# Batched rotary q·k scores on one core: twenty 2 MB loads change from SyncE's DMA ring to ScalarE's

## The chip, the cores and the metric

The kernel runs on one core of a Trainium2 chip (trn2). The metric is device time in microseconds, the median of three runs. The kernel before takes 792.87 us (792.67 to 793.26). A difference is read against that spread.

Words used below: PE is TensorE, DVE is VectorE, ACT is ScalarE, POOL is GpSimd, SP is SyncE. A DMA is issued by an instruction on SP, ACT or POOL, which puts it on that engine's ring (a queue); the core's 16 DMA engines then move the data. The profile calls SP's ring q1, ACT's q10 and POOL's q0. "To landing" is the time from the issue of a DMA until its last byte has arrived.

## The reference

For 16 batches of 512 positions, 16 heads and 64 elements, q and k are rotated with cos and sin of the position, and for every batch and head all 512 x 512 products are written out:

```python
q1, q2 = q[..., :half_dim], q[..., half_dim:]
q_rot = np.concatenate([q1 * cos_q - q2 * sin_q, q1 * sin_q + q2 * cos_q], axis=-1)
...
scores = np.einsum('bshd,bthd->bsht', q_rot, k_rot)
```

q and k are 33.5 MB each in fp32, the scores 268.4 MB. The kernel reads 67.24 MB and writes 268.44 MB, so four fifths of its traffic are stores.

## The kernel before

A batch is cut into C = 4 chunks of 128 positions (positions p*4 + c for chunk c), and each step i of 64 makes the scores of one chunk of q against all 512 positions of k of its batch. A step writes one staging tile st of 128 x 16 x 512 fp32 (4 MB) from eight pairs of heads. For each pair (`scores`, L190 on) PE makes two matrices of 128 x 512 in PSUM (L201), and ACT copies both to st (L208). After the eighth pair, SP issues the store of the whole tile (L188). There are three staging tiles, so the copies of step i can begin only when the store of step i - 3 has landed.

The inputs arrive by batch: `load` (L113) takes a tile of 128 x 4 x 1024 fp32 (2 MB) from `in_pool`, which has two buffers for q and two for k, and issues the load into it (L122). DVE rotates one chunk at a time in place (`rope`, L149, L150 and L154). PE transposes it by 128 x 128 blocks (L170). DVE copies the transposed q out of PSUM, and ACT the transposed k (L185).

The order of the work on each engine is the order in which the program issues it (`manual_schedule`). The first four steps have a loop of their own, with smaller loads and stores. From step 4 on, one step is:

```python
for p in range(HP):
    scores(i, p, st)
    ...
run(dve)
if i % C == C - 2:
    load("q", i // C + 2)
elif i % C == C - 1:
    load("k", i // C + 3)
```

Between the pairs of heads stand the transposes: at p = 1 and 3 those of q for step i + 1, at p = 5 and 6 those of k for step i + 4. So in each group of four steps one q load is issued after the third step's store and one k load after the fourth's, all on SP, behind the stores of the steps before. A load may be issued when PE has transposed the last chunk of the batch that was in its buffer; that happens within the step that the load follows, before its last pair of heads.

Five loads (q of batches 6, 11, 15 and k of batches 7 and 12) are special (`RELIEVED`, `load_around`, L86 on): POOL issues 120 of their 128 partitions so that one DMA engine is passed over. The other 8 partitions go by SP (L111, for q) or POOL (for k). The tiny transfers into `scratch` (L84) only move POOL's place among the DMA engines.

Of the kernel before, what the change touches and what calls it, by code (L numbers as in the profile page):

```python
# [10 lines left out]
def kernel(  # L11
# [8 lines left out]
    nc = tc.nc  # L20
# [4 lines left out]
    B, S, H, D = q.shape  # L25
    HD = D // 2
    P = 128
    C = S // P
# [14 lines left out]
    dram = {  # L43
        "q": q.rearrange("b (p c) h d -> b p c h d", c=C),
        "k": k.rearrange("b (p c) h d -> b p c h d", c=C),
    }
# [15 lines left out]
    def load_units(which, head, heads):  # L62
        n = C * heads * D
        t = early[:, used[0] : used[0] + n].rearrange("p (c e) -> p c e", c=C)
        used[0] += n
        src = dram[which][0, :, :, head : head + heads, :]
        nc.sync.dma_start(t.rearrange("p c (h d) -> p c h d", d=D), src)
        for h in range(0, heads, G):
            units[which, (head + h) // G] = t[:, :, D * h : D * (h + G)]
# [16 lines left out]
    def load_around(which, b, t):  # L86

        n, E, F = 120, C * H * D, C * H * D // 2  # L90
        x = RELIEVED[which, b]
        d = dram[which][b]

        def halves(lo, hi):
            src = bass.AP(d.tensor, d.offset + lo * E + F, [(E, hi - lo), (-F, 2), (1, F)])
            v = t[lo:hi].rearrange("p c e -> p (c e)")
            dst = bass.AP(v.tensor, v.offset + F, [v.ap[0], (-F, 2), (1, F)])
            nc.gpsimd.dma_start(dst, src)  # L98

        if x == 0:  # L100
            nc.gpsimd.inc_swdge_sem([], [], mode="reset_dge_cursor")
        else:

            move_cursor(16 - SLOW)
        if x % 2:
            move_cursor(8)
            halves(n, P)
        move_cursor(SLOW + 1)
        halves(0, n)
        if not x % 2:  # L110
            nc.sync.dma_start(t[n:].rearrange("p c (h d) -> p c h d", h=H), d[n:])  # L111

    def load(which, b):  # L113

        if b >= B:
            return
        t = in_pool.tile([P, C, H * D], fp32, tag=which + "_in", name=which + "_sb")
        batches[which, b] = t
        if (which, b) in RELIEVED:
            load_around(which, b, t)  # L120
        else:
            nc.sync.dma_start(t.rearrange("p c (h d) -> p c h d", h=H), dram[which][b])  # L122

    def rope(which, n):

        part = part_pool.tile([P, H * D], fp32, tag="part", name="part")
        if n < C:
            x = units[which, n]
            sv, k1, k2 = "p c (g j) -> p c g j", {"j": HD}, {"j": D}  # L130
            cs = cos_t.unsqueeze(2).to_broadcast((P, C, 2 * G, HD))
            ss = ss_v.unsqueeze(2).to_broadcast((P, C, G, D))
            pv = part.rearrange("p (c g j) -> p c g j", c=C, j=D)
            x5 = x.rearrange("p c (h x j) -> p c h x j", x=2, j=HD)
            p5 = part.rearrange("p (c h x j) -> p c h x j", c=C, x=2, j=HD)
            adds = [(x5[:, :, :, y], p5[:, :, :, 1 - y]) for y in range(2)]
        else:
            x = batches[which, n // C][:, n % C]
            sv, k1, k2 = "p (g j) -> p g j", {"j": HD}, {"j": D}
            cs = cos_t[:, n % C].unsqueeze(1).to_broadcast((P, 2 * H, HD))  # L140
            ss = ss_v[:, n % C].unsqueeze(1).to_broadcast((P, H, D))
            pv = part.rearrange(sv, **k2)
            x4 = x.rearrange("p (h x j) -> p h x j", x=2, j=HD)
            swapped = bass.AP(part.tensor, part.offset + HD, [part.ap[0], (D, H), (-HD, 2), (1, HD)])
            adds = [(x4, swapped)]
        xs, xc = x.rearrange(sv, **k2), x.rearrange(sv, **k1)

        def products():
            nc.vector.tensor_tensor(pv, xs, ss, op=mult)  # L149
            nc.vector.tensor_tensor(xc, xc, cs, op=mult)  # L150

        def sums():
            for y, z in adds:
                nc.vector.tensor_tensor(y, y, z, op=add)  # L154

        return [products, sums]
# [33 lines left out]
    def scores(i, p, st):  # L190

        ps = ps_s_pool.tile([P, 2, S], fp32, tag="ps_s", name="ps")
        b = i // C
        if b == 0:
            c, hp = divmod(p, 2)
            lhs, rhs = qT[i][:, C * hp + c], kT[0][:, 2 * i + hp]
        else:
            lhs, rhs = qT[i][:, p], kT[b][:, p]
        for r in range(2):
            po, rh = ps[:, r, :], rhs[64 * r : 64 * r + 64, :]  # L200
            nc.tensor.matmul(  # L201
                out=po, lhsT=lhs[64 * r : 64 * r + 64, :], rhs=rh, start=True, stop=True
            )
        so, si = st[:, 2 * p : 2 * p + 2, :], ps
        if b > 0:
            so = so.rearrange("s r (t c) -> s r t c", c=C)
            si = si.rearrange("s r (c t) -> s r t c", c=C)
        nc.scalar.copy(out=so, in_=si)  # L208
        if b == 0 and p % 2 == 1:
            c = p // 2  # L210
            nc.sync.dma_start(o_v[0, c, :, G * i : G * (i + 1)], st[:, G * c : G * (c + 1)])
        elif b > 0 and p == HP - 1:
            store(i, st)

    def tr_act(which, n):
        for g in range(2):
            transposed(which, n, g, nc.scalar.copy)

    def run(ops):
        for op in ops:  # L220
            op()

    with tc.manual_schedule():
        for t, src in ((cos_t, cos), (sin_t, sin)):
            nc.scalar.dma_start(t, src.rearrange("(p c) j -> p c j", c=C))
        for head, heads in ((0, G), (G, H - G)):
            load_units("k", head, heads)
            load_units("q", head, heads)
        load("k", 1)
        load("q", 1)  # L230
        make_identity(nc, ident)
        nc.scalar.copy(out=ss_t[:, :, 0, :], in_=sin_t)
        nc.scalar.mul(ss_t[:, :, 1, :], sin_t, -1.0)
        for which in ("k", "q"):
            run(rope(which, 0))
            tr_act(which, 0)

        for i in range(C):
            st = st_first[i] if i < 2 else stage_pool.tile([P, H, S], fp32, tag="stage", name="st")  # L240
            if i < C - 1:
                dve = rope("k", i + 1) + rope("q", i + 1) + rope("k", C + i)
                nxt = [("k", i + 1), ("q", i + 1)]
            else:
                dve = rope("q", C) + rope("k", C + i) + rope("q", C + 1) + rope("k", 2 * C)
                nxt = [("q", C), ("k", C + i)]
            for p in range(HP):
                scores(i, p, st)
                if p in (0, 1) and i > 0:
                    run(dve[:1])  # L250
                    dve = dve[1:]
                    transposed("k", C + i - 1, p, nc.vector.tensor_copy)
                if p == 3 and i < 2:
                    load("kq"[i], 2)
                if p in (2, 6):
                    m = len(dve) - (4 if p == 2 else 2) - (2 if i == C - 1 else 0)
                    run(dve[:m])
                    dve = dve[m:]
                    tr_act(*nxt.pop(0))
            run(dve)  # L260
        load("k", 3)

        for i in range(C, NST):
            tr = {}
            if i + 1 < NST:
                tr[1], tr[3] = ("q", i + 1, 0), ("q", i + 1, 1)
            if i + C < NST:
                tr[5], tr[6] = ("k", i + C, 0), ("k", i + C, 1)
            dve = []  # L270
            if i + 2 < NST:
                dve += rope("q", i + 2)
            if i + 1 + C < NST:
                dve += rope("k", i + 1 + C)
            st = stage_pool.tile([P, H, S], fp32, tag="stage", name="st")
            for p in range(HP):
                scores(i, p, st)
                if p not in tr:
                    continue
                if tr[p][0] == "q":  # L280
                    run(dve[:1])
                    dve = dve[1:]
                    transposed(*tr[p], nc.vector.tensor_copy)
                else:
                    transposed(*tr[p], nc.scalar.copy)
            run(dve)
            if i % C == C - 2:
                load("q", i // C + 2)
            elif i % C == C - 1:
                load("k", i // C + 3)  # L290

# [28 lines left out]
```

## Time and profile before

| what | value |
|---|---|
| median of three runs | 792.87 us |
| span of the profiled execution, first to last instruction | 790.4 us |
| median less span | 2.5 us |
| PE busy | 684.4 us (87%) |
| ACT busy | 562.0 us (71%) |
| DVE busy | 544.7 us (69%) |
| POOL busy | 11.9 us (2%) |
| moved by DMA | 336.18 MB, mean 425 GB/s |
| issues on SP: stores of 4 MB (L188) | 60, median 24.7 us to landing |
| issues on SP: k loads and q loads of 2 MB (L122) | 13 and 12, median 28.3 and 26.5 us to landing |
| issues on POOL: q and k of 1920 KB | 3 and 2, median 27.8 and 43.3 us to landing |

How to read it: busy time says how much an engine ran, not whether its work was what the end waited for. An engine that waits part of the time but is late with nothing costs nothing. The DMA part of a page gives the busy share of the 16 DMA engines and what they moved, in 40 equal slices of 19.76 us. The waits give, for each engine and line, how long it sat idle and what ended that. A table by stretches gives the same sums between two chosen moments. Issuing a DMA isn't counted as busy time of the engine that issues it; its duration stands in the timeline, as a row of SPq or ACTq.

### The profile page before, as it was taken

How to read it: one execution, taken by the hardware profiler on the slowest of the kernel's cores; microseconds unless marked ns; L12 is line 12 of the kernel's file. 1: busy time of each engine (PE TensorE's matmuls, PEld its weight loads, DVE VectorE, ACT ScalarE, POOL GpSimd, SP SyncE). 2: the span in 40 equal slices, each digit the busy share in tenths (PEclk: the TensorE clock that was granted, in tenths of full speed). 3: DMA queues.
4: the chain of work that ended last, by engine and by line, in shares of the span. 5: the costliest groups of instructions: out<-in, count | busy, mean ns of one | idle time of the engine just before them, and what ended most of it. 6: DMA issues, size and time to landing. Idle time of an engine off the chain costs nothing.

```text
span 790.4 us, 7750 instructions
## 1 busy us (share of the span) xinstructions
PE 684.4 (87%) x3072; PEld 296.4 (38%) x3072; DVE 544.7 (69%) x516; ACT 562.0 (71%) x647; POOL 11.9 (2%) x24
## 2 busy tenths in 40 slices
PE   4989998988988889798996989889899798799960
PEld 2444443433433334343342433334334343344420
DVE  6999988666766678576785767667678487587400
ACT  3888886865857768486785866777577586588770
POOL 0000000000001000000000001000000000000000
PEclk9999999998999999898998989999899899899995
DMA  9999999999999999999999999999999999999997
GB/s 357 417 425 439 429 430 435 425 435 436 429 429 428 413 432 419 433 423 438 433 427 436 426 432 429 422 432 424 430 432 427 436 429 432 430 432 434 432 429 340
DMA packets 18836, 336.18 MB, mean 425 GB/s; under 512 B 2312, under 2 KB 3592, under 8 KB 4616
## 3 DMA queue, kind: packets, MB, share of 16 engines
q1 hardware_dynamic: 16704, 325.46, 96.4%
q0 software_dynamic: 1808, 10.10, 3.1%
q8 instruction: 24, 0.39, 0.2%
q10 hardware_dynamic: 288, 0.13, 0.1%
q14 instruction: 12, 0.10, 0.0%
HBM read 67.24 MB, written 268.44 MB: 425 GB/s over the span
## 4 chain that ended last, share of the span: by engine, by line
DMA 49%; PE 40%; ACT 5%; DVE 3%; issue 1%; ACTq 0%; SPq 0%; DVEq 0%
DMA out_dram<-st 46%; PE ps L201 30%; PE bank L170 10%; ACT st L208 5%; DMA q_sb<-in_q_dram 2%; DVE part L149 1%; DMA early<-in_k_dram 1%; DVE q_sb L150 0%; DVE k_sb L154 0%; DVE k_sb L150 0%; DVE q_sb L154 0%; DVE early L150 0%; DVE kT_t L185 0%; ACTq L316 0%; DVE early L154 0%
## 5 line engine op out<-in xcount | busy, mean ns | idle before, releaser
L208 ACT COPY st<-ps 128x1024 f32<-128x1024 f32 x512 | 495.7, 1020 | 192.6 <-DMA out_dram<-st 109.8
L201 PE MATMUL ps<-kT_t,qT_t 64*128 64x512 f32 x2048 | 544.0, 649 | 67.0 <-ACT st L208 67.0
L201 PEld LDWEIGHTS ps<-kT_t,qT_t 64*128 64x128 f32 x2048 | 183.6, 196 | 256.2 <-issue 133.3
L185 DVE COPY qT_t<-bank 128x512 f32<-128x512 f32 x118 | 81.6, 691 | 193.9 <-PE bank L170 193.9
L170 PEld LDWEIGHTS bank<-ident,q_sb 128*128 128x128 f32 x480 | 54.2, 149 | 99.0 <-issue 96.4
L170 PEld LDWEIGHTS bank<-ident,k_sb 128*128 128x128 f32 x480 | 50.3, 140 | 96.4 <-DVE k_sb L150 39.5
L170 PE MATMUL bank<-ident,q_sb 128*128 128x128 f32 x480 | 85.1, 304 | 0.9 <-PE ps L201 0.9
L170 PE MATMUL bank<-ident,k_sb 128*128 128x128 f32 x480 | 78.5, 286 | 1.6 <-DVE qT_t L185 1.2
L185 ACT COPY kT_t<-bank 128x512 f32<-128x512 f32 x122 | 72.4, 598 | 6.4 <-PE bank L170 6.4
L154 DVE TENSOR_TENSOR k_sb<-k_sb,part 128x1024 f32<-128x1024 f32 x60 | 73.5, 1225 | 2.1
L150 DVE TENSOR_TENSOR q_sb<-q_sb,cos_t 128x1024 f32<-128x1024 f32 x60 | 73.5, 1225 | 2.1
L150 DVE TENSOR_TENSOR k_sb<-k_sb,cos_t 128x1024 f32<-128x1024 f32 x60 | 73.5, 1225 | 2.0
L149 DVE TENSOR_TENSOR part<-q_sb,ss_t 128x1024 f32<-128x1024 f32 x60 | 73.5, 1225 | 2.0
L149 DVE TENSOR_TENSOR part<-k_sb,ss_t 128x1024 f32<-128x1024 f32 x60 | 73.0, 1216 | 0.9 <-DMA k_sb<-in_k_dram 0.7
L154 DVE TENSOR_TENSOR q_sb<-q_sb,part 128x1024 f32<-128x1024 f32 x60 | 72.9, 1216 | 0.0
L170 PE MATMUL bank<-ident,early 128*128 128x128 f32 x64 | 10.5, 315 | 12.4 <-DVE early L154 10.5
L170 PEld LDWEIGHTS bank<-ident,early 128*128 128x128 f32 x64 | 8.3, 161 | 17.4 <-issue 13.4
L149 DVE TENSOR_TENSOR part<-early,ss_t 128x1024 f32<-128x1024 f32 x8 | 9.8, 1222 | 5.8 <-DMA early<-in_k_dram 5.7
L98 POOL DMA_DIRECT2D q_sb<-in_q_dram x3 | 2.3, 752 | 620.2 <-PE bank L170 446.2
L154 DVE TENSOR_TENSOR early<-early,part 128x512 f32<-128x512 f32 x16 | 10.3, 687 | 0.2
L150 DVE TENSOR_TENSOR early<-early,cos_t 128x1024 f32<-128x1024 f32 x8 | 9.8, 1225 | 0.3
L185 ACT COPY qT_t<-bank 128x512 f32<-128x512 f32 x10 | 5.7, 629 | 3.2 <-PE bank L170 3.2
(12 smaller groups left out, 15.9 us busy)
## 6 DMA issues: line engine op xcount, KB each, us to landing
out_dram<-st SPq DMA_DIRECT2D x60, 4096.0 KB, 24.7
k_sb<-in_k_dram SPq DMA_DIRECT2D x13, 2048.0 KB, 28.3
q_sb<-in_q_dram SPq DMA_DIRECT2D x12, 2048.0 KB, 26.5
out_dram<-st SPq DMA_DIRECT2D x16, 1024.0 KB, 13.8
q_sb<-in_q_dram POOLq DMA_DIRECT2D x3, 1920.0 KB, 27.8
k_sb<-in_k_dram POOLq DMA_DIRECT2D x2, 1920.0 KB, 43.3
early<-in_k_dram SPq DMA_DIRECT2D x1, 1536.0 KB
early<-in_q_dram SPq DMA_DIRECT2D x1, 1536.0 KB
```

What stands on the lines that cost most here:

```text
L98: nc.gpsimd.dma_start(dst, src)
L149: nc.vector.tensor_tensor(pv, xs, ss, op=mult)
L150: nc.vector.tensor_tensor(xc, xc, cs, op=mult)
L154: nc.vector.tensor_tensor(y, y, z, op=add)
L170: nc.tensor.transpose(bank[:, x, :], src, ident)
L185: copy(out=dst, in_=src)
L201: nc.tensor.matmul(out=po, lhsT=lhs[64 * r : 64 * r + 64, :], rhs=rh, start=True, stop=True)
L208: nc.scalar.copy(out=so, in_=si)
```

## The change

`load` gets a third argument, the queue on which its DMA is issued, with SP's as its default. The two calls in the loop over steps 4 to 63 pass ACT's queue. The loads issued before that loop, `load("k", 1)`, `load("q", 1)`, `load("kq"[i], 2)` and `load("k", 3)`, keep the default, and a load in `RELIEVED` takes the branch of `load_around` as before. The loop's calls ask for batches 3 to 15 of q and 4 to 15 of k, and those past the last batch return at once. Less the five in `RELIEVED`, 20 loads of 2 MB are issued by ACT instead of SP. ACT meets each in its own order: behind the eighth copy of the step, and ahead of the first copy of the next.

```diff
-    def load(which, b):
+    def load(which, b, queue=nc.sync):
...
         if (which, b) in RELIEVED:
             load_around(which, b, t)
         else:
-            nc.sync.dma_start(t.rearrange("p c (h d) -> p c h d", h=H), dram[which][b])
+            queue.dma_start(t.rearrange("p c (h d) -> p c h d", h=H), dram[which][b])
...
             if i % C == C - 2:
-                load("q", i // C + 2)
+                load("q", i // C + 2, nc.scalar)
             elif i % C == C - 1:
-                load("k", i // C + 3)
+                load("k", i // C + 3, nc.scalar)
```

## The prediction

> **What bounds the kernel now.** I read the busy shares first, then the DMA rows, the waits, and last the stretches in which a second ring was already active. The page on the DMA:
>
> ```profile
> DMA  9999999999999999999999999999999999999997
> GB/s 357 417 425 439 429 430 435 425 435 436 429 429 428 413 432 419 433 423 438 433 427 436 426 432 429 422 432 424 430 432 427 436 429 432 430 432 434 432 429 340
> ...
> q1 hardware_dynamic: 16704, 325.46, 96.4%
> q0 software_dynamic: 1808, 10.10, 3.1%
> ...
> q10 hardware_dynamic: 288, 0.13, 0.1%
> HBM read 67.24 MB, written 268.44 MB: 425 GB/s over the span
> ```
>
> The 16 DMA engines are busy in every slice, while PE, the busiest of the compute engines, shows 87% and ACT 71%. Nearly all bytes go over q1, SyncE's ring; q0 is GpSimd's; q10, with only cos and sin on it, is ScalarE's. The rate by stretch (the last two columns are the DMA share and GB/s):
>
> ```profile
> 160.00:180.00 20.00, 17.25 (x77) 7.29 (x75) 13.26 (x13) 13.06 (x16) 0.00 (x0) 0.91 1.01 432
> 226.00:246.00 20.00, 17.15 (x66) 6.90 (x66) 12.60 (x12) 12.26 (x15) 1.88 (x3) 0.83 1.01 432
> 475.00:495.00 20.00, 17.28 (x82) 7.28 (x80) 14.00 (x13) 13.02 (x16) 3.01 (x5) 1.00 1.01 430
> 246.00:266.00 20.00, 18.76 (x90) 8.15 (x91) 15.04 (x16) 15.92 (x19) 3.01 (x5) 1.00 1.01 415
> 500.00:520.00 20.00, 18.20 (x78) 7.72 (x80) 14.06 (x14) 14.00 (x17) 0.00 (x0) 0.91 1.01 417
> 300.00:310.00 10.00, 10.00 (x50) 4.43 (x48) 8.55 (x8) 8.77 (x11) 0.00 (x0) 1.00 1.00 408
> 700.00:780.00 80.00, 63.61 (x300) 27.09 (x296) 32.98 (x33) 57.74 (x65) 0.00 (x0) 0.93 1.00 432
> ```
>
> 432 GB/s is what stores alone reach (700 to 780), and loads in one ring with stores reach it too (160 to 180). 336.18 MB at 432 GB/s take 778 us; the span is 790.4. Of the 12.2 us between, the first slice of 19.76 us (357) costs 3.4, the second (417) 0.7 and the last (340) 4.2, all outside the part that changes. Some 3.9 us are left for the whole middle. That is the most that any other order of the same bytes could give back.
>
> The waits say the same: ScalarE waits for old stores to land, DVE hardly ever for a load.
>
> ```profile
> ACT st L208 <- DMA out_dram<-st: 109.8, 42, 5.7
> DVE part L149 <- DMA k_sb<-in_k_dram: 0.7, 1, 0.7
> SPq L122 <- PE bank L170: 4.8, 6, 0.8
> SPq L122 <- PE ps L201: 3.4, 14, 0.3
> ```
>
> A load that lands sooner therefore serves nobody. The period of four steps: four stores of 4.19 MB and two loads of 2.10 MB at 432 GB/s are 4 x 9.71 + 2 x 4.85 = 48.5 us, and the stores issued at 354.80 and 403.27, four steps apart, are 48.47 us apart. Compute alone needs 4 x 10.0 us (stores issued at 113.76, 123.77, 133.79).
>
> **The change part by part.** Twenty loads move (q of batches 3 to 15 without 6, 11, 15; k of batches 4 to 15 without 7 and 12): 41.9 MB. GpSimd's five, with the small remainder of q that SyncE issues at L111, stay. q1 should fall from 325.46 to 283.5 MB and q10 rise to 42.1. No byte and no packet is added.
>
> *Issue, on SyncE.* Today:
>
> ```profile
> 133.79 0.33 SPq L188 DMA_DIRECT2D out_dram<-st  x1
> 134.23 0.55 SPq L122 DMA_DIRECT2D q_sb<-in_q_dram  x1
> 149.20 0.33 SPq L188 DMA_DIRECT2D out_dram<-st  x1
> 149.63 0.53 SPq L122 DMA_DIRECT2D k_sb<-in_k_dram  x1
> ```
>
> The load is issued 0.44 us after its step's store, and the next store comes 15 or 10 us later. SyncE gains nothing by being rid of it: 0.
>
> *Issue, on ScalarE.* The load stands behind the eight copies of its step. Its buffer's last readers, the transposes at positions 1 and 3 (q) or 5 and 6 (k), ran before the last matmul that these copies need, so I expect no true wait: the waits for PE on SyncE were 0.8 us at most. The issue itself is bounded below by ScalarE's own two (0.38 and 0.45 us for cos and sin), above by SyncE's longest load (1.25): 20 x 0.38 to 1.25 = 8 to 25 us of ScalarE. Behind it are queued the copies of the next step. After the q load they wait anyway: ScalarE idles 4.8 us at 133.8 and 4.1 us at 183.8 until a store lands. After the k load they don't (the copies at 148.16 run on), so 10 x 0.38 to 1.25 = 4 to 12 us of stores issued later. The cover is the stores still queued in the DMA engines: one takes 24.7 us from issue to landing and only 9.7 us of transfer, so about 15 us of work lies ahead of it. Cost 0; without the cover, up to 12 us.
>
> *Order in the DMA engines.* Now the load waits behind two or more stores (26.5 us to landing for q, 28.3 for k). On its own ring it alternates with them. GpSimd's ring does so today: in 230 to 240 us its 8 KB packets moved 0.84 MB, 84 of 431 GB/s, a fifth, as one packet of 8 KB against one of 32 KB would. With 16 KB against 32 KB the load gets a third, 144 GB/s, and lands in 14.6 us, about 15 with the issue. The stores that are open in that time get two thirds and land up to 4.85 us later. ScalarE waits longer for these and less for the next ones, since the load is by then out of the way. The work ahead of the engines stays the same, so the time stays too, as long as they always have some. Sum: 0.
>
> *Rate while two rings are active.* This is the only term with a size. For a single load in the second ring the nearest rows are 226 to 246 (432: 0 us lost in 20), 475 to 495 (430: 0.09) and 670 to 690 (427: 0.23): 0.1 us a load, 2 us for twenty. GpSimd's packets are of half the size, though (312 ns for 8 KB, 617 for 16 KB, which is already 0.05 us a load). I take a quarter, +0.5 us. The upper end is a whole q and k pair on GpSimd's ring with what follows it: (432 - 415) / 432 x 20 = 0.8 us in 246 to 266, 0.3 in 266 to 286 (426), about 1 us a pair, +10 us for ten. The lower end: the stretches below rate in the middle (0.8 + 0.3, 0.7 in 500 to 520, 0.55 in 300 to 310, the last under SyncE's ring alone) vanish, -2.3 us.
>
> The Trainium skill has a rule that speaks against the change: "DMA: Bandwidth & Descriptors", section "Rules for kernel authors", says that spreading DMAs over the issuing engines does not help bandwidth, because they all run on the same 16 engines and interleave, and saves only issue time. By it the sum is exactly 0 and the time 792.9; the rows at 432 agree with it, those at 415 and 417 would make it +7 to +10.
>
> Sum: 790.4 + 0.5 = 790.9 us of span. The median shown, 792.87, is 2.5 us above this execution's span; with that, **793.4 us**.
>
> **Rivals.**
> 1. *Mixing costs* (slower). Loads among stores for 20 x 14.6 us bring the stretches of 415 and 417 with them. For: both stand where GpSimd's k load runs. Against: the 408 of 300 to 310 has no second ring, and 226 to 246 has one and loses nothing. Between 0.1 us a load and 1 us a pair, at 0.15 to 0.2 a load: +3 to +4, 796.
> 2. *Leading engines run dry* (slower, one place: the first step after a landing). With the load drawn forward, only two stores are queued when a buffer comes free: 2 x 9.71 = 19.4 us. The landing comes up to 1.4 us after the last packet (the last packet ends at 789.0, the span at 790.4). One DMA engine lags: by the packet records it starts its share of the k load of 200.78 at 222.6, the first engine at 217.8, 4.8 us apart. So the leaders run dry when the step takes over 19.4 - 1.4 - 4.8 = 13.2 us. The longest I found is 187.97 to 199.95, 12.0; with an issue of 1.25 on ScalarE it just reaches the point. Leaders cannot lose more than the lead before the laggard bounds: +4, 797. Against: most such steps take 10.7 (138.54 to 149.20), and most engines are within 1.5 us of each other.
> 3. *Mixing evens out* (faster). The slow stretches, which contain loads each time, thin out: -2.3 us, 790.5. Against: the 700 to 780 rate is already met in most of the middle.
> 4. *It does not do what it says*: a wait on ScalarE puts the load where it was. The load then lands as late as today, 792.9; this counts as no change.
>
> **How the numbers follow.** 0.2% of 792.87 is 1.6 us, about what a measurement of this kernel can tell from no change: within is 791.3 to 794.5. My forecast gets 0.48 and rival 4 0.05, rival 1 0.20, rival 2 0.13, rival 3 0.14. Faster 0.14, within 0.53, slower 0.33. The range goes from rival 3 (790.5) past rivals 1 and 2 to 798.5; the full +10 (803) is left out. The forecast's own range is 791.5 to 794.5.
>
> **What would show it.** Right: q10 at 42.1 MB and about 12.6% of the engines' span (20 x 128 x 0.617 us / 16 = 99 us), q1 at 84%; ACTq loads of 2048 KB landing in about 15 us, stores somewhat over 24.7; ScalarE's wait for out_dram near 110 us, less the issues; every middle slice of GB/s still 413 to 439. Rival 1: DMA share still 1.0 with the rate at 415 to 425 in stretches with ACTq loads. Rival 2: DMA digits or shares below 0.99 in the middle. Wrong altogether: DVE waiting for q_sb or k_sb, or ScalarE idle before L122 for microseconds.

## The result and the profile after

The changed kernel takes 799.05 us, the median of five runs (797.59 to 799.99), against 792.87 before: a ratio of 1.0075, 95% interval 1.0062 to 1.0087. It is 6.2 us slower, where 0.5 us had been forecast, and half a microsecond past the upper end of the range. The execution profiled has a span of 798.2 us and took 799.99.

The page of the kernel after, its part on the DMA: busy tenths and GB/s in 40 slices of 19.96 us, then the queues (packets, MB, share of the 16 engines' time).

```profile
DMA  9999999999999999999999999999999999999996
GB/s 349 391 426 434 433 428 436 420 429 429 424 433 424 430 415 429 427 420 434 422 431 441 422 433 419 428 412 424 432 424 421 433 416 432 423 432 427 437 429 296
...
q1 hardware_dynamic: 13824, 283.51, 83.7%
q10 hardware_dynamic: 3168, 42.08, 12.5%
...
HBM read 67.24 MB, written 268.44 MB: 421 GB/s over the span
```

The bytes moved from q1 to q10 as predicted, and the engines are as busy as before, yet they move less per microsecond. To see where, take the table by stretches, in order: the stretch and its length, busy time of PE, PEld, DVE, ACT and POOL, PE's clock, DMA share, GB/s. First the kernel before, in two long stretches in the middle, then the kernel after in the same two, and below them in pieces of these with the moved loads in flight (340 to 370, 635 to 665) and almost without (370 to 390, 615 to 635; the load before each of these ends at 373 and 619).

```profile
320.00:410.00 90.00, 81.02 (x360) 34.84 (x360) 62.76 (x59) 67.06 (x77) 0.00 (x0) 0.92 1.01 432
585.00:665.00 80.00, 71.28 (x328) 30.67 (x326) 58.82 (x55) 58.93 (x68) 0.00 (x0) 0.96 1.00 430
```

```profile
320.00:410.00 90.00, 80.53 (x352) 34.40 (x352) 62.58 (x59) 65.23 (x75) 0.00 (x0) 0.91 1.00 428
585.00:665.00 80.00, 70.17 (x310) 29.61 (x306) 54.78 (x52) 55.94 (x64) 0.00 (x0) 0.92 1.00 425
340.00:370.00 30.00, 24.29 (x114) 10.16 (x110) 19.88 (x19) 20.13 (x24) 0.00 (x0) 0.93 1.00 423
370.00:390.00 20.00, 19.91 (x92) 8.60 (x90) 15.27 (x14) 15.63 (x19) 0.00 (x0) 0.94 1.01 433
635.00:665.00 30.00, 25.31 (x118) 10.57 (x114) 20.93 (x20) 21.16 (x25) 0.00 (x0) 0.96 1.00 420
615.00:635.00 20.00, 19.58 (x80) 8.46 (x82) 13.26 (x13) 15.65 (x19) 0.00 (x0) 0.83 1.01 434
```

Between the loads the engines move 433 and 434 GB/s, as much as before. While a q and a k load run on ScalarE's ring beside the stores, it is 423 and 420, at a DMA share of 1.00. So (432 - 423) / 432 x 30 = 0.6 us and (432 - 420) / 432 x 30 = 0.8 us are lost for each q and k pair; ten of them would make 6 to 8 us. This is rough, since a stretch counts a packet where it starts.

The records of single packets are finer and say less. (A packet is what one of the 16 engines moves at a time, 32 KB of a store or 16 KB of a load.) From 72 to 782 us a mean of 16.07 packets is open both before and after: the engines never run out of work. The median store packet of 32 KB takes 1213 ns in both, but the mean goes from 1219 to 1229: some packets take longer. What all packets take beyond the median of their size and queue, summed from 72 to 720 us and divided by the 16 engines, is 4.1 us before and 8.3 after. That is +4.2, and it is the stores' (2.9 us before, 7.2 after); the load packets lose 1.0 in both. The last of the 16 engines ends 2.4 us after their mean before, and 4.4 after: +2.0. That the two together make just the 6.2 us is in part luck, since the second is not tied to the change: it is 5.5 in run k_only below, which is as fast as the kernel before. (The spans of the two profiled executions differ by 7.8. The rest lies at 25 to 35 us, where this execution moved 363 GB/s and the one before 428, ahead of any moved load. Run after_rot below, as slow as the change, moved 429 there, so I don't count it to the change.)

### The profile page after: what moved, and what is told of

It is laid out like the page before. It is cut to its first block, busy times and chain, and to the rows that moved or that the text cites. A ratio compares the mean times of both kernels' runs of the same rounds, so it can differ in the third digit from the quotient of the medians.

```text
span 798.2 us, 7741 instructions
## 1 busy us (share of the span) xinstructions
PE 687.9 (86%) x3072; PEld 298.0 (37%) x3072; DVE 544.4 (68%) x516; ACT 562.4 (70%) x647; POOL 11.9 (1%) x24
## 3 DMA queue, kind: packets, MB, share of 16 engines
q10 hardware_dynamic: 3168, 42.08, 12.5%
## 4 chain that ended last, share of the span: by engine, by line
DMA 49%; PE 37%; DVE 5%; ACT 4%; issue 1%; ACTq 0%; DVEq 0%
DMA out_dram<-st 49%; PE ps L201 28%; PE bank L170 9%; ACT st L208 4%; DVE part L149 2%; DMA early<-in_k_dram 1%; DVE early L154 1%; DVE k_sb L154 1%; DVE k_sb L150 1%; DVE early L150 1%; DVE kT_t L185 0%; DVE q_sb L150 0%; DVE q_sb L154 0%; ACTq L316 0%; DVE qT_t L185 0%
## 6 DMA issues: line engine op xcount, KB each, us to landing
k_sb<-in_k_dram POOLq DMA_DIRECT2D x2, 1920.0 KB, 52.5
```

## The experiments

After the result two theories stood. *Issue*: what costs is that ScalarE, which has the copies to do, issues the loads. *Mixing*: what costs is that two rings are active at once. A third, *Order*, is that the loads now overtake stores, which then land later. Each experiment starts from the kernel before unless it says otherwise. `load` has the queue argument of the change wherever a diff passes `nc.scalar` to it.

### One half of the change alone

Only the q loads, which follow a step's store, or only the k loads, move.

```diff
-                load("q", i // C + 2)
+                load("q", i // C + 2, nc.scalar)      # run q_only
...
-                load("k", i // C + 3)
+                load("k", i // C + 3, nc.scalar)      # run k_only
```

> Only the ten q loads go by ScalarE's ring; the k loads stay on SyncE's. Mixing (packets take longer while loads and stores of two rings alternate on the DMA engines; 6.2 us for twenty loads, so 0.31 us each): about +3 us, 796. Issue (the time of the DMA instruction on ScalarE delays its copies): the q issue stands before a wait for a landing, so it costs nothing, 793. Order (the load overtakes stores and these land later): +3, 796.

Measured: 796.64 us (795.17 to 798.58), ratio 1.0051, 1.0038 to 1.0065.

> Only the ten k loads go by ScalarE's ring. Mixing: about +3 us, 796. Issue: all of the loss is here, since the copies behind the k load do not wait for a landing: +6, 799. Order: +3, 796.

Measured: 792.31 us (790.72 to 792.74), ratio 0.9987, 0.9979 to 0.9996.

None of the theories had both. The k loads, issued by ScalarE in front of copies that are ready to run, should have cost most by *issue*; they cost nothing. A price for each load, by *mixing* or *order*, should have come to 3 us with either half; one half pays 3.7 us and the other nothing. What differs is what they run beside. The landings of run k_only (KB each, median us from issue to landing):

```profile
q_sb<-in_q_dram SPq DMA_DIRECT2D x12, 2048.0 KB, 27.0
k_sb<-in_k_dram ACTq DMA_DIRECT2D x10, 2048.0 KB, 16.4
```

The k load is mostly issued some 9 us after a q load that waits behind two stores on SyncE's ring, and meets that q load. By the packet records, between 350 and 360 us q10 moved 206 GB/s, the load on q1 151 and stores only 74, at 431 in total. In run q_only the load on q10 runs beside stores. So a fourth theory, *company*: a second ring costs when it runs beside stores, and not beside a load.

### The issue by itself

Three runs leave all loads on SyncE. In two of them ScalarE also issues 20 DMAs of 128 bytes, where the moved loads would stand. The first puts them in a new tile; the second, in free columns of `scratch`, so that no tile moves; the third only moves the tiles.

```diff
-    scratch = const_pool.tile([P, 96], fp32, name="scratch")
+    scratch = const_pool.tile([P, 136], fp32, name="scratch")      # run shift, nothing else
...
+    marks = const_pool.tile([16, 40], fp32, name="marks")          # run tiny_act
...
+            src = bass.AP(q.tensor, 512 * y, [(512, 16), (1, 2)])
+            nc.scalar.dma_start(marks[:, 2 * y : 2 * y + 2], src)                    # run tiny_act
+            nc.scalar.dma_start(scratch[:16, 50 + 2 * y : 52 + 2 * y], src)          # run tiny_act2
```

> The loads stay on SyncE's ring; at each of the twenty places ScalarE issues a transfer of 128 bytes into a spare tile. It keeps the issue on ScalarE and its ring's second stream, without the bytes. Mixing: 793, no change. Order: 793. Issue: +6, 799.

Measured: 796.25 us (795.68 to 797.20), ratio 1.0045, 1.0033 to 1.0057. It looked like a price of issue, against what the half changes had shown. But the new tile of 160 bytes in each partition also moved every tile that is allocated after it, so the next two took it apart.

> The twenty issues of 128 bytes on ScalarE again, but into free columns of the existing spare tile, so that no other tile's address in SBUF moves (the spare tile of tiny_act moved them by 160 bytes a partition). Issue (the DMA instruction or the second ring's stream as such costs time): +3.5 us as in tiny_act, 796. Placement (the 160 bytes were the cause there): 793.

Measured: 793.77 us (792.19 to 795.44), ratio 1.0005, 0.9995 to 1.0014: the issue costs nothing that can be told.

> The kernel before with a spare tile that is 160 bytes a partition longer, nothing else; all loads on SyncE. Placement: +3.5 us, 796. Issue: 793, no change. If tiny_act2 and shift both come out at 793, it takes both together.

Measured: 795.56 us (794.94 to 797.03), ratio 1.0030, 1.0021 to 1.0039: the place alone costs 2.4 us. In the kernel before, the load tiles and the staging tiles start on multiples of 256 bytes in each partition; here they stand 160 bytes later. tiny_act was a flawed experiment, and what it measured was its tile.

### All on one ring

From the fifth step on the stores go to ScalarE's ring too, so that stores and loads share one ring again, another one. This starts from the kernel after.

```diff
-        nc.sync.dma_start(o_v[i // C, i % C], st)
+        nc.scalar.dma_start(o_v[i // C, i % C], st)
```

> As the changed kernel, but from the fifth step on the 4 MB stores go by ScalarE's ring too, so loads and stores stand in one ring again, in the order of the kernel before, and ScalarE issues eighty DMAs. Mixing: near 793. Order: near 793. Issue: four times as many issues, at least +6 and up to +25: 799 to 818. A small rise of 1 or 2 us would fit all, since ScalarE must see its last copy end before it issues the store.

Measured: 792.18 us (791.76 to 793.26), ratio 0.9995, 0.9986 to 1.0004. ScalarE now issues 80 large DMAs and the time is that of before. The page of this run, and its stretches:

```profile
q10 hardware_dynamic: 11808, 293.74, 86.8%
q1 hardware_dynamic: 5184, 31.85, 9.7%
```

```profile
320.00:410.00 90.00, 77.90 (x350) 33.31 (x352) 60.74 (x58) 64.80 (x74) 0.00 (x0) 0.94 1.01 433
585.00:665.00 80.00, 71.77 (x326) 30.44 (x324) 58.30 (x55) 58.84 (x69) 0.00 (x0) 0.96 1.00 431
```

The rate of 433 and 431 is back with the loads on the same ring as after. Neither ScalarE nor its ring is slow. *Issue* has fallen.

### Stores beside stores

All loads stay on SyncE. In the 20 steps that a moved load would follow, the store is cut in two by heads; the second half goes by ScalarE, or, as the control, by SyncE too.

```diff
-        nc.sync.dma_start(o_v[i // C, i % C], st)
...
+            nc.sync.dma_start(o_v[i // C, i % C][:, : H // 2], st[:, : H // 2])
+            nc.scalar.dma_start(o_v[i // C, i % C][:, H // 2 :], st[:, H // 2 :])    # run store_two_rings
+            nc.sync.dma_start(o_v[i // C, i % C][:, H // 2 :], st[:, H // 2 :])      # run store_one_ring
```

> All loads on SyncE's ring. In the twenty steps after which a load moved, the 4 MB store is issued in two halves of 2 MB, the second of them on ScalarE's ring: two rings are active as long as in the changed kernel, but with stores in both. To be read against store_one_ring. Direction (it is loads among stores that slow packets): no change against it, 793 to 794. Offsets (a second ring is entered by each DMA engine at another point of its own list, which changes the engines' distances, and what follows meets slow packets, whatever is in the ring): +4 to +6 us against it.

Measured: 802.93 us (801.42 to 810.24), ratio 1.0135, 1.0105 to 1.0164.

> The control to store_two_rings: the same twenty stores in two halves, both on SyncE's ring. All theories: within 1 us of the kernel before, 792 to 794, since the DMA engines run the same bytes in one list; packets of 16 KB in place of 32 KB cost 20 x 8 x (2 x 0.611 - 1.213) = 1.4 us at most.

Measured: 793.99 us (792.88 to 794.30), ratio 1.0008, 0.9999 to 1.0016.

The cut costs nothing, the second ring 8.9 us, though the loads stay on SyncE's ring. So the time does not need a load on the second ring. Where it is lost differs from the kernel after, as the profiled executions show (first three rows store_two_rings, then the control):

```profile
290.00:480.00 190.00, 168.66 (x746) 71.82 (x747) 132.05 (x125) 136.06 (x156) 1.80 (x3) 0.93 1.01 431
118.00:166.00 48.00, 40.28 (x182) 17.09 (x180) 32.08 (x31) 31.30 (x38) 0.00 (x0) 0.93 1.00 419
780.00:800.00 20.00, 0.00 (x0) 0.00 (x0) 0.00 (x0) 0.00 (x0) 0.00 (x0) 0.50 0.57 246
```

```profile
290.00:480.00 190.00, 170.02 (x758) 72.89 (x756) 134.91 (x126) 137.72 (x158) 1.88 (x3) 0.94 1.00 430
118.00:166.00 48.00, 43.91 (x204) 19.00 (x202) 36.13 (x35) 36.43 (x42) 0.00 (x0) 0.96 1.01 431
```

From 290 to 480, with eight store halves on ScalarE's ring, nothing is lost. The loss stands in some other stretches, such as 118 to 166, and at the end, where the engines are busy only 57%: one engine's last packet ends at 798.9 us, the next engine's at 792.7. Packets lose 7.8 us beyond their median, against 3.2 in the control. The pair differs in one thing more: with two rings SyncE issues the load ahead of ScalarE's half (at 332.7 and 337.9 us, for one), so that parts of some halves run beside SyncE's load. That reading beside writing has a part in the price is therefore not excluded. So a second ring with stores lengthens this kernel, but stores beside stores have no fixed price; what starts the loss, no run tells. Nor does one tell why one engine fell 6.2 us behind, where the next most is 3.8, in run k_late below.

### Order without a second ring

The loads stay on SyncE, but are issued after the seventh pair of heads, ahead of the store of their step, so that they overtake it.

```diff
+            nxt = {C - 2: ("q", i // C + 2), C - 1: ("k", i // C + 3)}.get(i % C)
...
+                if p == HP - 2 and nxt and nxt not in RELIEVED:
+                    load(*nxt)
...
+            if nxt in RELIEVED:
+                load(*nxt)
```

> All loads on SyncE's ring, but each of the twenty is issued ahead of its step's store instead of behind it, so that the load overtakes one store inside one ring. Order (a load that overtakes stores and delays their landing costs the time): at least half of the 6.2 us, 796 or more. Second ring (time is lost only where two rings are served at once and packets take longer): 793, the rate between 72 and 782 us near 429.7 GB/s as in the kernel before.

Measured: 793.25 us (791.48 to 794.05), ratio 1.0005, 0.9996 to 1.0014. The landings of this run, and two of its waits:

```profile
k_sb<-in_k_dram SPq DMA_DIRECT2D x13, 2048.0 KB, 19.6
q_sb<-in_q_dram SPq DMA_DIRECT2D x12, 2048.0 KB, 21.3
```

```profile
ACT st L208 <- DMA out_dram<-st: 110.1, 37, 6.3
DVE part L149 <- DMA k_sb<-in_k_dram: 16.7, 2, 8.9
```

The loads land 5 to 9 us sooner than before (26.5 and 28.3), k sooner than in the kernel after and q 1 us later, and the time stays. That a load overtakes a store costs nothing here: *order* has fallen.

### The k load beside stores

The direct test of *company*: only the k loads move, as in k_only, but each is issued one step later, when the q load is through and only stores run.

```diff
+            elif i % C == 0 and i > C and ("k", i // C + 2) not in RELIEVED:
+                load("k", i // C + 2, nc.scalar)
```

> As k_only (k on ScalarE's ring, q on SyncE's), but each k load is issued one step later, when the q load of SyncE's ring has been served. In k_only the two loads of a group ran beside each other; here k runs beside stores. Company (a load costs what it costs by running beside stores of the other ring; beside a load it is free): +3 us against k_only, 795 to 796. Which tensor or which place in the group it is, not the company: as k_only, 792 to 793.

Measured: 796.41 us (794.59 to 800.20), ratio 1.0058, 1.0038 to 1.0078. The same ten loads on the same ring cost nothing beside a load (k_only) and 3.7 us beside stores. *Company* holds for loads, as to when the price is due. Where it is paid is another matter. The execution profiled took 799.46 us, 3 us over its kernel's median, so its losses are larger than usual. The GB/s of this run in 40 slices of 19.94 us, and three stretches:

```profile
GB/s 348 425 428 435 431 421 435 429 432 439 419 427 431 421 431 419 437 421 427 437 428 434 396 437 429 408 427 435 428 428 425 442 395 426 397 432 435 431 431 301
```

```profile
315.00:330.00 15.00, 7.20 (x32) 2.92 (x32) 7.15 (x7) 5.73 (x8) 0.00 (x0) 0.78 1.01 436
350.00:360.00 10.00, 10.00 (x50) 4.41 (x49) 8.55 (x8) 8.67 (x11) 0.00 (x0) 1.00 1.00 411
438.00:458.00 20.00, 20.00 (x100) 8.86 (x96) 16.62 (x16) 17.34 (x21) 0.00 (x0) 1.00 1.00 406
```

From 315 to 330 a k load runs on q10 beside stores at the full rate. The loss is in later stretches, 350 to 360 and 438 to 458, where a q load is served from SyncE's own ring. By the packet records, count what all packets that start while a load runs take beyond the median of their size and queue, in engine-us (16 of them, one on each engine, are 1 us of the kernel). It is 0.9 for a load on q10 here and 6.4 for a q load on q1; before, a load has 0.8 in the mean. Run q_only is the same with the parts exchanged: 2.1 for the q loads on q10, 5.0 for the k loads on q1. In both, nearly all of the loss on q1 is in the load's own packets. In the kernel after, where no such load is on q1, the 20 on q10 have 4.0 each: 20 x (4.0 - 0.8) / 16 = 4.0 us more than before. Here the longer packets are those of the stores beside the load (3.2 of the 4.0). So the change pays at once and in the stores, the half changes later and in the next load.

### Addresses, and time beside stores

Two more, from the kernel after. In the first, each moved load reads the batch eight further on (16 MB away), so that those batches' scores are of other inputs. In the second, each moved load is cut in two by chunks, with packets of 8 KB for 16.

```diff
-            queue.dma_start(t.rearrange("p c (h d) -> p c h d", h=H), dram[which][b])
+            queue.dma_start(t.rearrange("p c (h d) -> p c h d", h=H),
+                            dram[which][b if queue is nc.sync else (b + 8) % B])     # run after_rot
...
+            for c in (0, 2) if queue is nc.scalar else ():                           # run after_8k
+                queue.dma_start(v[:, c : c + 2], src[:, c : c + 2])
```

> The changed kernel, but the twenty loads on ScalarE's ring read the batch eight further on (16 MB away in HBM), so the scores of these batches are those of other batches. Company: the same as the changed kernel, 797 to 800. Addresses (the slow packets come from where in HBM the loads and the stores beside them lie): a clear change, 793 or up to 805.

Measured: 799.02 us (796.35 to 799.75), ratio 1.0075, 1.0062 to 1.0088. Equal to the change: it isn't a matter of which addresses meet, as far as this one shift shows it.

> The changed kernel, but each of the twenty loads is issued as two DMAs of 1 MB with packets of 8 KB in place of 16 KB. Beside stores of 32 KB packets the load then gets a fifth instead of a third of the engines and stays beside them for about 24 us in place of 14.6. Company with a price by time: 6.2 x 24 / 14.6 = +10 us, 803; packets of 8 KB alone add 20 x 8 x (2 x 0.309 - 0.611) = 1 us. Company with a price by load or by byte: 799 to 800.

Measured: 802.62 us (799.91 to 810.03), ratio 1.0139, 1.0106 to 1.0173, 9.9 us over before against 6.2. With packets of half the size the loads take a fifth of what the engines move (19 to 20% by the packet records, against a third) and so last longer beside the stores, and the price grows by 3.6 us. About 1 us of this is that two packets of 8 KB take longer than one of 16 KB, as the expectation worked out. The runs of this kernel spread over 10 us, so the size of the growth is rough.

## Why the prediction was wrong, step by step

**What bounds the kernel: right.** The DMA engines bound it, before and after. The share of 1.00 and the 16.07 packets open say so.

**Issue on SyncE, 0, and on ScalarE, 0: right.** The issue took 0.33 us each time, below the bounds, and the waits that it needed were met. ScalarE's timeline after (start, us, engine, line, work; idle time before it in brackets):

```profile
138.51 1.01 ACT L208 COPY st<-ps 128x1024 f32<-128x1024 f32 x1
138.52 0.34 ACTq L122 DMA_DIRECT2D q_sb<-in_q_dram  x1
140.16 3.76 ACT L208 COPY st<-ps 128x1024 f32<-128x1024 f32 x4 [0.64 <-DVE q_sb L150]
...
148.61 0.33 ACTq L122 DMA_DIRECT2D k_sb<-in_k_dram  x1
153.83 2.84 ACT L208 COPY st<-ps 128x1024 f32<-128x1024 f32 x3 [4.29 <-DMA out_dram<-st]
```

The load is issued while the copy ahead of it still runs. Behind this k load ScalarE waits 4.29 us for a store anyway. tiny_act2 (1.0005) and all_act (0.9995) confirm both zeros.

**Order in the DMA engines, 0: right in its cost, partly wrong in its picture.** The load takes about a third of the rate as worked out: by the packet records a q load's transfer lasts 14 to 16 us where 14.6 had been expected. But the first packet starts 2.6 to 4.5 us after the issue, and the k load is issued while the q load is still running on the same ring, so that its first packet comes 5.5 to 8.5 us after. Hence the landings:

```profile
out_dram<-st SPq DMA_DIRECT2D x60, 4096.0 KB, 25.3
q_sb<-in_q_dram ACTq DMA_DIRECT2D x10, 2048.0 KB, 20.3
k_sb<-in_k_dram ACTq DMA_DIRECT2D x10, 2048.0 KB, 24.9
```

I had forecast 15 for both. The waits for the loads and the stores, after:

```profile
ACT st L208 <- DMA out_dram<-st: 114.0, 44, 7.0
DVE part L149 <- DMA k_sb<-in_k_dram: 17.1, 2, 8.7
```

ScalarE's wait is near the 110 forecast. DVE's two waits for a k tile, which I had named as a sign that the prediction is wrong altogether, are there: they are for GpSimd's k loads, which land after 52.5 us instead of 43.3. They cost nothing. Runs k_only (16.8) and early_sp (16.7) have them too, at the time of before.

**Rate while two rings are active, +0.5: this step failed.** The term was the right one and its size was wrong. The time rose by 6.2 us, some 0.3 us a load, within the term's own bounds (-2.3 to +10); of this the packets show +4.2 as lost rate. I took a quarter of the 0.1 us a load that I read from stretches in which one load of GpSimd ran beside stores, because GpSimd's packets are of half the size. The packets' own times gave half of it for that (0.05 us a load), and no row gave the rest of the reduction; in after_8k smaller packets beside the same stores cost more, and not only by their own times. Nor was that row the right one. A stretch that ends with its load misses what is paid later: run k_late shows the full rate while the rings mix and 406 to 411 in the next load. The row of a pair with what follows it, which I had put at about 1 us and used only as the upper end, was the nearer one; after the change a pair costs about 0.6 us by the total. That it holds two loads is not the point, since single loads pay as much: 3.7 us for ten in q_only and in k_late. The fall to 408 at 300 to 310 us of the kernel before, which I took as evidence against *Mixing costs* because only SyncE's ring was at work, is the first of SyncE's loads after a pair by GpSimd. The packets that start while it runs lose 6.0 engine-us; the first load after GpSimd's second pair has 2.2, and the other 18 have 0.1 to 1.1. That fits a price paid late; I had read it as a loss without a second ring.

**The rivals.** Rival 1, *Mixing costs*, is what happened, and its 0.15 to 0.2 us a load (796) was still too little. Its "loads among stores" is too wide: loads among stores on one ring cost nothing (all_act, early_sp), loads that run beside a load of the other ring cost nothing (k_only), and a second ring that carries only stores costs too, in some stretches (store_two_rings). Rival 2, *Leading engines run dry*, would show as a lower DMA share; there is none. Rival 3's -2.3 did not come, and rival 4 is excluded by q10's 42.08 MB.

**The rule.** I weighed the Trainium skill's "DMA: Bandwidth & Descriptors", section "Rules for kernel authors", that spreading DMAs over the issuing engines doesn't help bandwidth and saves only issue time. The runs agree that it doesn't help. That it is neutral, as I read it, they don't show: in this kernel it costs 0.75%, and 0.13% is the most that a second ring gave back (k_only).

**What stays open.** That loads on a second ring beside stores make some packets longer is shown, by rate and by packet. Why isn't. One picture would be that the 16 engines work off one ring in fixed distances from each other, and that a second ring shifts these distances, so that packets meet others until the distances have settled. Before, the spread of the engines' ends of one DMA does stay at 3.8 to 4.0 us from 320 to 410 us, and for a store it swings between 5.6 and 9.4 after. But in store_two_rings the ends of SyncE's DMAs lie 9.7 to 14.6 us apart in the same stretch and change from one to the next, and nothing is lost there. So shifting distances alone are not enough, and the cause stays open.

## What to carry to other kernels

Where the DMA engines are full, as here, try first to keep stores and the loads among them on one ring, whichever engine issues it; if a second ring is needed, let its loads meet the other ring's loads and not its stores. This one kernel shows it; another has to be measured. When a cost is bounded by rows of the profile, take the row with the same sequence of transfers, and look at the stretch after it too. When a test needs a tile, put it where no other tile moves.

## What the runs showed of the hardware

- A ring of loads and stores runs equally fast from SyncE and from ScalarE (0.9995, 0.9986 to 1.0004), and 20 issues on a ScalarE that is 71% busy are free (1.0005).
- Half of each of 20 stores on a second ring cost 1.35% here, against 0.08% for the same halves on one ring, though 190 us of it ran at the full 431 GB/s. The lowest ratio of the study is k_only's: 0.13% faster than before (0.9979 to 0.9996), less than the 0.2% that I had named as the least that can be told from no change, though its interval leaves 1 out.
- The tiles' place counts: 160 bytes more ahead of them cost 0.30%. The Trainium skill's "DMA: Bandwidth & Descriptors", section "How a descriptor splits into AXI transactions", says that a transaction that reads must begin at a multiple of 256 bytes and that a start in between costs extra. The time agrees in sign, the packets don't: the median store packet, which reads the tile, stays at 1213 ns, and the stores lose 2.8 us beyond it against 2.9. It is some of the load packets, which write the tile, that are longer (3.6 us beyond their median against 1.0).
